# A two-layer decoder trunk on one core: the latent attention's moves between tiles leave by GpSimd's DMA queue

## The chip, the cores and the metric

The kernel runs on one core of one Trainium2 chip. A core has five instruction streams that run side by side and are tied together by semaphores: TensorE (PE, matmuls; its weight loads are listed as PEld), VectorE (DVE), ScalarE (ACT), GpSimd (POOL) and SyncE (SP). Each stream runs its instructions in the order in which the program was built. SP does no arithmetic here: it only issues DMAs. A DMA is issued by the stream on which it stands; the 16 DMA engines of the core then move the bytes.

The metric is device time in microseconds (us) of one execution of the whole program, as the median of several runs.

## The reference, cut to what matters

Two layers; in each layer one projection of the residual stream `x` (512 tokens x 1024) feeds four branches that are gated, projected, merged and normalised:

```python
for l in range(DEPTH):                      # DEPTH = 2
    h = x @ w_in[l]
    (rw_p, rw_g, q_lat, kv_lat, k_pe, mla_g, conv_u, conv_g, xq, xg, merge) = split(h)
    y_rwkv = _rwkv7_branch(...)             # recurrence, 8 heads x 64
    y_mla  = _mla_branch(q_lat, kv_lat, k_pe, mla_g, ...)
    y_conv = _conformer_conv_branch(conv_u, conv_g, ...)   # width 31
    y_mem  = _memory_xattn_branch(xq, xg, mem, ...)
    merged = sum(sigmoid(merge_n + b_n) * (y_n @ w_o_branch[l, n]) for n in 4 branches)
    x = layer_norm(alpha * x + merged @ w_out[l])
```

The branch that the change touches is the latent attention:

```python
q  = (rms_norm(q_lat) @ w_uq).reshape(S, 8, 64 + 32)     # per head: plain part, rotary part
kv = (rms_norm(kv_lat) @ w_ukv).reshape(S, 8, 64 + 64)   # per head: key part, value
q_pe, k_pe = rope(q_pe), rope(k_pe)                      # k_pe is shared by all heads
q_full = concat([q_nope, q_pe]); k_full = concat([k_nope, k_pe])      # 96 rows per head
o = causal softmax attention over 128-query blocks
```

Everything is float32. The kernel gets this accuracy from faster matmuls by splitting each operand into a high part (`h`, rounded to the float32r type) and a low part (`l`, the rest), and adding three products (`mm3`).

## The kernel before, in words

**Who decides the order.** The program is one stream of work items for PE (the projections, `stream`), into which side tasks are mixed (splitting weights, attention blocks, the convolution's taps, the recurrence). A class `Plan` keeps a clock for each engine while the program is being built. Each instruction gets a cost, and a task goes on as soon as the planner's clock of PE has reached the task's time; otherwise the next piece of the stream is put out. So the costs written into `Plan` fix the order in which instructions stand on every engine, and a change of a cost moves instructions far away from it. On the chip each engine then follows that order and waits where the planner was wrong.

**Weights.** `weights` issues one DMA of up to 128 x 1024 numbers from SP (`DMA`, which books `Plan.dma`) into one of two raw buffers (`WR = 2`), then a task splits it: ACT writes the high part, DVE the low part, into one of six pairs of tiles (`WH = 6`). The names `w0`, `w1`, ... count these pieces, so `w25h` and `w25l` are the parts of the 26th. `LOOK = 4` halves are fetched ahead. The next weights' DMA can go only when a raw buffer is free, that is, when the split of the piece that was in it has ended.

**The latent attention.** `lat_item` projects the latents, `latents` normalises and transposes them (`lt`). `key_rotary` rotates the shared key part, splits it into `krh` and `krl` and has it moved to rows 64 to 95 of the four key tile pairs `kTh`, `kTl` (8 moves in each layer). `latent_items` then makes the rotary query parts of all heads (`pqe`, `query_rotary`, transposed as `qr`, split as `qrh`, `qrl`), the values (`pv`), and four items `pair_item(hh)`, each for two heads. A pair item has the rotary parts of its queries moved to rows 64 to 95 of the query tiles `qT`, `qTl` (4 moves), computes the plain parts (`pq` for queries, `pk` for keys), and `heads` splits these (`xqh`, `xql`, `xkh`, `xkl`) and has each half moved to rows 0 to 63 of the tiles of its head (8 moves). In all 56 moves in each layer. They all go from SBUF to SBUF, since an engine's lanes keep their partitions.

When the moves of a pair are there, `pair` starts eight blocks (`mla_block`, at most three open at a time): scores `ms`, a maximum, the exponential and its sum, normalisation `mP`, transposes `mt`, a copy `mPT`, and after every four blocks the products with the values, `mo`.

**What is queued where.** Before the change, moves and weights share SP's queue. SP takes its DMAs in order: one that waits for its source, or for the DMA eight places before it that used the same semaphore, holds back those behind it. POOL runs small operations only: the reciprocal roots of the norms (`rstd_of`) and the substitution of the recurrence (`ZT`, `tmpW`).

**The convolution's norm.** `conv_norm` writes a tanh (`ctn`) into a tile of the general pool `up` (32 tiles of 128 x 512), and DVE multiplies it into `yc`. The pool `sp` has a tag `tg` with two buffers, used by the tanh of all the gates.

**Other names of the profile.** `ps_m`, `po`: projections of the merge gates and of the branches; `ps_glu`, `ps_val`, `cacc`: the convolution; `xs`, `xt`, `xo`: the cross-attention; `ps_xq`: its queries, which also go through tiles named `xqh`, `xql`; `ps_mk`, `pmv`: its keys and values; `pz`: the output projection.

Of the kernel before, what the change touches and what calls it, by code (L numbers as in the profile page):

```python
# [10 lines left out]
F32 = mybir.dt.float32  # L11
# [55 lines left out]
class Plan:  # L67
# [52 lines left out]
    def dma(self, size, outs, ins):  # L120
        t = max(self.queue, self.start("DMA", [n for n in outs if self.done.get(n, ("", ""))[1] != "DMA"], ins)) + (420.0 if ins[0][:3] == "in_" else 590.0)
        self.queue = t
        self.wires = max(self.wires, t + 650.0) + size / 360.0
        self.end("DMA", self.wires + 1500.0, outs, ins)

    def slot(self, key, bufs, name):

        q = self.slots.setdefault(key, [])
        q.append(name)
        if len(q) > bufs:  # L130
            self.done[name] = (self.seen.get(q.pop(0), 0.0), "")
# [67 lines left out]
def _names(*aps):  # L199
    return [a.tensor.name for a in aps if hasattr(a, "tensor")]  # L200
# [65 lines left out]
def trunk_kernel(ctx: ExitStack, tc: tile.TileContext, A, out, dbg=None):  # L266
    nc = tc.nc
    plan = Plan(tc.keep_in_program_order)
# [19 lines left out]
    def TR(o, i):  # L288
        plan.shape(128, 128)
        plan.op("PE", 109.0, _names(o), _names(i))  # L290
        plan.keep(nc.tensor.transpose(o, i, ident))  # L291

    def DMA(o, i, name=None):
        n = 512
        for d in o.shape[1:]:
            n *= d
        plan.dma(n, [name] if name else _names(o), _names(i))
        plan.keep(nc.sync.dma_start(o, i))

    def pool(bufs, **k):  # L300
        return Space(plan, ctx.enter_context(tc.tile_pool(bufs=bufs, **k)), bufs)
# [5 lines left out]
    sp = pool(2, name="sp")  # L307
# [18 lines left out]
    def u(name, cols=512, dt=F32, p=128):  # L326
        return up.tile([p, cols], dt, tag="u", name=name)

    def st(name, cols, bufs=8, dt=F32):
        return sp.tile([128, cols], dt, tag=f"st{cols}", name=name, bufs=bufs)  # L330
# [133 lines left out]
    def free(n=1):  # L464
        wlive["hl"] -= n
# [70 lines left out]
    HALF = [slice(0, 64), slice(64, 128)]  # L536
# [61 lines left out]
    def layer_items(l):  # L598
        items = []
        L = {}  # L600
        t_ = f"_{l}"
# [534 lines left out]
        def conv_norm():  # L1136
            ntok = []
            yield lambda: added[3] == 8
            for tb in range(4):
                ps, = yield from pa.take([128, 512], f"ct{tb}" + t_)  # L1140
                for i in range(4):
                    TR(ps[:, 128 * i:128 * i + 128], cacc[i][:, 128 * tb:128 * tb + 128])
                yield
                bs, mv = st(f"cbs{tb}" + t_, 6), st(f"cmv{tb}" + t_, 2)
                V.bn_stats(bs, ps)
                V.bn_aggr(mv, bs)
                rs = st(f"crs{tb}" + t_, 1)
                rstd_of(rs, mv[:, 1:2], 1.0, LN_EPS)
                n = u(f"cn{tb}" + t_)
                V.tensor_scalar(out=n, in0=ps, scalar1=mv[:, 0:1], scalar2=rs, op0=ALU.subtract, op1=ALU.mult)  # L1150
                pa.free()
                ntok.append(n)
                yield
            yield lambda: added[1] >= 4
            for i in range(4):
                ps, = yield from pa.take([128, 512], f"cb{i}" + t_)
                plan.due(*ntok)
                yield "pe"
                for tb in range(4):
                    TR(ps[:, 128 * tb:128 * tb + 128], ntok[tb][:, 128 * i:128 * i + 128])  # L1160
                yield
                t, z = u(f"ctn{i}" + t_), u(f"yc{i}" + t_)
                S.activation(t, ps, AF.Tanh, scale=hp("cln_g", i), bias=hp("cln_b", i))
                V.tensor_scalar(out=z, in0=ps, scalar1=pr("cln_g", i), scalar2=pr("cln_b", i), op0=ALU.mult, op1=ALU.add)
                pa.free()
                V.scalar_tensor_tensor(out=z, in0=t, scalar=1.0, in1=z, op0=ALU.add, op1=ALU.mult)
                yconv.append(z)
                yield
# [130 lines left out]
        def key_rotary():  # L1299

            kpe, ts = L["kpe"], u("rk" + t_, 256)
            k4 = kpe.rearrange("p (a d) -> p a d", a=4)
            yield lambda: angles
            rope(k4[:, :, 0:16], k4[:, :, 16:32], [ts[:, 64 * i:64 * i + 64].rearrange("p (a d) -> p a d", a=4) for i in range(4)], lambda f: f)
            ps, = yield from pa.take([128, 512], "kr" + t_)
            plan.due(kpe)
            yield "pe"
            for tb in range(4):
                TR(ps[0:32, 128 * tb:128 * tb + 128], kpe[:, 32 * tb:32 * tb + 32])
            yield  # L1310
            kr = [sp.tile([32, 512], F32R, tag="mt", name=f"kr{n}" + t_) for n in "hl"]
            yield from split(*kr, ps[0:32])
            pa.free()
            plan.due(*kr)
            yield
            for kT in L["kT"]:
                for x, y in zip(kT, kr):
                    DMA(x[64:96].bitcast(F32), y.bitcast(F32))
                plan.t += 2000.0
                yield  # L1320

# [28 lines left out]
                latT.append((h, lo))  # L1350

        ymla = []
        L["pe"] = L["pairs"] = L["jobs"] = L["turn"] = 0
        qpe, vtok = [], []

        def token_blocks(get, ks, name, cols, after):
# [59 lines left out]
        def pair_item(hh):  # L1416
            def run(get):
                wq = yield from get()
                wk = yield from get()
                there = []  # L1420
                qT = [(m(f"qT{hh}{h}" + t_, 512, "lq", 4, 96, F32R),
                       m(f"qTl{hh}{h}" + t_, 512, "qo", 1, 96, F32R) if hh % 2 > h else
                       u(f"qTl{hh}{h}" + t_, 512, F32R, 96) if hh % 2 else m(f"qTl{hh}{h}" + t_, 512, "qp", 2, 96, F32R)) for h in range(2)]
                kT = [L["kT"][2 * (hh % 2) + h] for h in range(2)]
                for h in range(2):
                    r = 64 * (hh % 2) + 32 * h
                    for x, y in zip(qT[h], qpe[hh // 2]):
                        DMA(x[64:96].bitcast(F32), y[r:r + 32].bitcast(F32), f"qTpe{hh}{h}" + t_)
                for w, ks, T, n, s in ((wq, range(3), qT, "q", MSCALE), (wk, range(3, 5), kT, "k", 1.0)):
                    ps = pp.tile([128, 512], F32, tag="pp", name=f"p{n}{hh}" + t_)  # L1430
                    for i, k in enumerate(ks):
                        c = slice(128 * i, 128 * i + 128)
                        mm3(ps, w[0][:, c], w[1][:, c], latT[k][0], latT[k][1], i == 0, k == ks[-1])
                        yield
                    free()
                    plan.spawn(heads(T, ps, n, s, there))
                plan.spawn(pair(hh, qT, kT, there))
            item([(A["w_qk"][l, hh], (384, 256))], run,
                 lambda: len(latT) == 5 and len(qpe) > hh // 2 and len(vtok) == 4 and L["pairs"] >= hh - 1 and MEM[l] is not None)

        def heads(T, ps, n, s, there):

            parts = [u(f"x{n}{x}" + t_, 512, F32R) for x in "hl"]
            S.activation(parts[0], ps, AF.Copy, scale=s)
            V.scalar_tensor_tensor(out=parts[1], in0=ps, scalar=s, in1=parts[0].bitcast(F32), op0=ALU.mult, op1=ALU.subtract)
            plan.due(*parts)
            yield
            for i, x in enumerate(parts):
                for h in range(2):
                    y = T[h][i]  # L1450
                    DMA(y[0:64].bitcast(F32), x[HALF[h]].bitcast(F32), f"{n}{i}{h}" + y.tensor.name)
                    there.append(f"{n}{i}{h}" + y.tensor.name)

        def pair(hh, qT, kT, there):
# [16 lines left out]
        def mla_block(hh, h, i, T, mo, two, done, left):  # L1471


            n = 128 * i + 128
# [18 lines left out]
                TR(ps[:, 128 * kb:128 * kb + 128], P[:, 128 * kb:128 * kb + 128])  # L1493
            yield

            if i > 1:
                PT = m("mPT" + q, 512, "mPT", 4)
            else:
                if h not in two:
                    two[h] = m("mPT" + q, 512, "mPT", 4)  # L1500
                PT = two[h][:, 128 * i:]
# [8 lines left out]
            for b in (i - i % 2, i - i % 2 + 1):  # L1510
                for kb in range(b + 1):
                    for half in range(2):
                        MM(mo[HALF[half], 128 * b:128 * b + 128], vtok[kb][:, 128 * hh + 64 * half:128 * hh + 64 * half + 64],
                           two[half, b][:, 128 * kb:128 * kb + 128], start=kb == 0, stop=kb == b)
            left[0] -= 1
            if left[0] == 0:
                L["pairs"] += 1
# [504 lines left out]
```

## Time and profile before

| | us |
|---|---|
| median of 3 runs | 1519.35 |
| lowest, highest | 1518.24, 1521.86 |
| span of the profiled execution, first to last instruction | 1518.1 |
| median less span | 1.25 |
| POOL busy, whole span | 135.8 |
| mean granted TensorE clock | 0.997 |
| DMA queue of SP | 151.65 MB in 88880 packets |

The profiled execution has no time of its own besides its span; the runs' times are taken without a profile, so the 1.25 us between span and median also hold the difference of one run from another.

How to read it: a row of the windows gives, for one stretch of time, the busy microseconds of each engine with the number of its instructions in brackets, then the granted TensorE clock as a share of full speed, the share of time in which the 16 DMA engines were busy, and GB/s. A row of the waits says who waited for whom, for how long in total, how often, and the longest. A row of the timeline starts with the start and the duration, and may end with the idle time before it and what ended that. `L235`, `L286`, `L291` and `L298` are the lines of the helpers that record each operation, each matmul, each transpose and each DMA, so instructions are told apart by their tiles: `out<-in`.

### The profile page before, as it was taken

The page shows a single profiled execution, that of the slowest core. Times are in us where ns is not written, and L with a number is a line of the kernel's source. Part 1 is how long each engine was busy: PE and PEld are TensorE (multiplying, and loading weights), DVE is VectorE, ACT ScalarE, POOL GpSimd, SP SyncE. Part 2 cuts the span into 40 slices and gives each one's busy share as a digit, 9 for nine tenths or more (in the row PEclk, how much of TensorE's full clock was granted, in tenths as well). Part 3 has the DMA queues.
Part 4 walks back from the last instruction along what each step waited for, and adds up shares of the span by engine and source line. Part 5 has one row for each costly group of instructions (what it writes and reads, how often), then busy time and mean ns, then how long its engine had stood idle before and what let it go on. Part 6 is the DMA issues. An engine that isn't in the chain of part 4 may idle for free.

```text
span 1518.1 us, 29700 instructions
## 1 busy us (share of the span) xinstructions
PE 1485.7 (98%) x11896; PEld 1238.0 (82%) x11896; DVE 1072.7 (71%) x2231; ACT 686.6 (45%) x1499; POOL 135.8 (9%) x323
## 2 busy tenths in 40 slices
PE   8999999999999999999999999999999999999997
PEld 8877788887887878888999877888887878788886
DVE  5788988765757675555554889997766586756747
ACT  5535653445245453344255556533443545443432
POOL 0000000030402021000010000000030303120002
PEclk9999999999999999999999999999999999999999
DMA  6443333322232323433343252433232323235231
GB/s 211 124 113 93 104 100 98 98 85 83 74 93 60 94 74 93 139 98 114 123 146 114 81 125 69 121 107 97 81 99 61 93 64 93 69 95 181 98 116 65
DMA packets 89018, 153.54 MB, mean 101 GB/s; under 512 B 41008, under 2 KB 47152, under 8 KB 88880
## 3 DMA queue, kind: packets, MB, share of 16 engines
q1 hardware_dynamic: 88880, 151.65, 33.9%
q8 instruction: 93, 1.52, 0.4%
q14 instruction: 45, 0.37, 0.1%
HBM read 134.32 MB, written 5.77 MB: 92 GB/s over the span
## 4 chain that ended last, share of the span: by engine, by line
PE 89%; DVE 5%; DMA 2%; ACT 2%; issue 1%; SPq 1%; POOL 0%; ACTq 0%; DVEq 0%; POOLq 0%
PE ps_m L286 22%; PE po L286 11%; PE ps_cg L286 3%; PE ps_rg L286 3%; PE ps_v L286 3%; PE ps_xg L286 3%; PE ps_mg L286 3%; PE ps_k L286 3%; PE ps_r L286 3%; PE ps_val L286 3%; PE pz L286 2%; PE ms L286 2%; PE pl L286 2%; PE ps_glu L286 2%; PE ps_xq L286 2%; PE x L286 2%
## 5 line engine op out<-in xcount | busy, mean ns | idle before, releaser
L235 DVE SCALAR_TENSOR_TENSOR cacc<-hpad,prm,cacc 128x512 f32<-128x512 f32 x240 | 178.9, 748 | 3.3
L235 ACT ACTIVATE tm<-ps_m,prm 128x512 f32<-128x512 f32 x64 | 44.1, 689 | 148.5 <-PE ps_m L286 134.7
L235 DVE SCALAR_TENSOR_TENSOR mt<-tm,po 128x512 f32<-128x512 f32 x48 | 33.0, 687 | 79.2 <-PE po L286 79.1
L235 POOL TENSOR_SCALAR ZT<-W 64x256 f32<-64x256 f32 x8 | 4.8, 600 | 621.8 <-DMA W<-scr 287.7
L235 POOL TENSOR_TENSOR ZT<-ZT,tmpW 64x14 f32<-64x14 f32 (+6 forms) x112 | 44.0, 393 | 8.8
L235 ACT ACTIVATE mP<-ms,nmm 128x512 f32<-128x512 f32 (+3 forms) x64 | 33.7, 529 | 18.3 <-DVE nmm L235 17.4
L235 POOL TENSOR_TENSOR tmpW<-ZT,W 64x14 f32<-64x14 f32 (+6 forms) x112 | 39.9, 356 | 7.9
L235 ACT COPY mPT<-mt 128x512 f32<-128x512 f32 (+3 forms) x64 | 26.7, 429 | 22.4 <-PE mt L291 17.1
L235 DVE TENSOR_TENSOR merged<-merged,mt 128x512 f32<-128x512 f32 x48 | 33.8, 704 | 1.6
L235 DVE TENSOR_REDUCE nmm<-ms 128x1 f32<-128x512 f32 (+3 forms) x64 | 29.9, 483 | 0.6 <-PE ms L286 0.2
L235 POOL TENSOR_SCALAR gr<-gm 128x8 f32<-128x8 f32 x8 | 2.3, 286 | 311.2 <-DVE gm L235 311.2
L291 PE MATMUL mt<-cst,mP 128*128 128x128 f32 x160 | 27.1, 276 | 2.6 <-DVE mP L235 2.2
L235 DVE SCALAR_TENSOR_TENSOR merged<-tm,po 128x512 f32<-128x512 f32 x16 | 11.0, 687 | 22.0 <-PE po L286 20.3
L235 DVE TENSOR_SCALAR mP<-mP,smm 128x512 f32<-128x512 f32 (+3 forms) x64 | 24.8, 387 | 2.3
L235 ACT ACTIVATE yb<-yb,mr,gr 128x64 f32<-128x64 f32 x64 | 22.1, 430 | 9.0 <-DVE mr L235 9.0
L235 POOL TENSOR_SCALAR lrs<-lmv 128x1 f32<-128x1 f32 x8 | 2.5, 315 | 263.5 <-DVE lmv L235 261.8
L291 PEld LDWEIGHTS mt<-cst,mP 128*128 128x128 f32 x160 | 18.6, 141 | 8.2 <-ACT mo L235 2.2
L235 ACT ACTIVATE z<-z,lnb,lrs 128x256 f32<-128x256 f32 (+1 forms) x16 | 9.6, 647 | 31.2 <-DVE lnb L235 31.2
L286 PE MATMUL ms<-kTl,qT 96*128 96x512 f32 (+3 forms) x64 | 22.2, 347 | 0.0
L286 PE MATMUL mo<-mPT,v 128*64 128x128 f32 x320 | 21.4, 278 | 0.5 <-ACT mPT L235 0.5
L286 PE MATMUL ms<-kTh,qT 96*128 96x512 f32 (+3 forms) x64 | 20.6, 322 | 0.0
L286 PEld LDWEIGHTS mo<-mPT,v 128*64 128x64 f32 x320 | 17.3, 136 | 4.0 <-issue 2.9
(3535 smaller groups left out, 5323.2 us busy)
## 6 DMA issues: line engine op xcount, KB each, us to landing
w<-in_w_ch_dram SPq DMA_DIRECT2D x146, 512.0 KB, 3.6
w<-in_w_o_dram SPq DMA_DIRECT2D x32, 512.0 KB, 3.6
w<-in_w_out_dram SPq DMA_DIRECT2D x16, 512.0 KB, 3.6
w<-in_w_lat_dram SPq DMA_DIRECT2D x16, 336.0 KB, 3.3
w<-in_w_mk_dram SPq DMA_DIRECT2D x8, 512.0 KB, 3.5
w<-in_w_mv_dram SPq DMA_DIRECT2D x8, 512.0 KB, 3.5
w<-in_w_qk_dram SPq DMA_DIRECT2D x8, 320.0 KB, 3.1
x<-in_xT_dram SPq DMA_DIRECT2D x8, 256.0 KB, 5.6
```

What stands on the lines that cost most here:

```text
L235: return self.plan.keep(f(*a, **k))
L286: plan.keep(nc.tensor.matmul(o, lhsT, rhs, start=start, stop=stop))
L291: plan.keep(nc.tensor.transpose(o, i, ident))
```

## The change

Four edits. `Plan` gets a second kind of DMA, `move`, which books 1000 ns on POOL's clock and lands the bytes some time after that; like `dma`, it does not order itself after other DMAs into the same tile. A function `MOVE` issues it from `nc.gpsimd`. The three places that move parts of queries and keys between tiles call `MOVE`. The tanh of the convolution's norm takes its tile from `sp`, tag `tg`. And a counter `L["values"]` counts the groups of `mo` products put out; a block waits, before it takes its tile for the transposed probabilities, until the groups of earlier pairs, and for the last block of a pair the first group of its own, have been put out.

```diff
+    def move(self, size, outs, ins):
+        t = self.start("POOL", [n for n in outs if self.done.get(n, ("", ""))[1] != "DMA"], ins) + 1000.0
+        self.clk["POOL"] = t
+        self.end("DMA", t + size / 180.0 + 1900.0, outs, ins)
...
+    def MOVE(o, i, name=None):
+        n = 512
+        for d in o.shape[1:]:
+            n *= d
+        plan.move(n, [name] if name else _names(o), _names(i))
+        plan.keep(nc.gpsimd.dma_start(o, i))
...
-                t, z = u(f"ctn{i}" + t_), u(f"yc{i}" + t_)
+                t, z = sp.tile([128, 512], F32, tag="tg", name=f"ctn{i}" + t_), u(f"yc{i}" + t_)
...
-                    DMA(x[64:96].bitcast(F32), y.bitcast(F32))
+                    MOVE(x[64:96].bitcast(F32), y.bitcast(F32))
...
-        L["pe"] = L["pairs"] = L["jobs"] = L["turn"] = 0
+        L["pe"] = L["pairs"] = L["jobs"] = L["turn"] = L["values"] = 0
...
-                        DMA(x[64:96].bitcast(F32), y[r:r + 32].bitcast(F32), f"qTpe{hh}{h}" + t_)
+                        MOVE(x[64:96].bitcast(F32), y[r:r + 32].bitcast(F32), f"qTpe{hh}{h}" + t_)
...
-                    DMA(y[0:64].bitcast(F32), x[HALF[h]].bitcast(F32), f"{n}{i}{h}" + y.tensor.name)
+                    MOVE(y[0:64].bitcast(F32), x[HALF[h]].bitcast(F32), f"{n}{i}{h}" + y.tensor.name)
...
+            if i != 2 and L["values"] < 2 * hh + i // 2:
+                yield lambda: L["values"] >= 2 * hh + i // 2
             if i > 1:
                 PT = m("mPT" + q, 512, "mPT", 4)
...
+            L["values"] += 1
             left[0] -= 1
```

In the built program 112 DMAs leave SP's list and stand on POOL's, and the order on PE, DVE and ACT differs from PE's 259th matmul row on.

## The prediction

> **What bounds the kernel now.** First the page: its busy shares, its slices and the engine shares of its chain.
>
> ```profile
> PE 1485.7 (98%) x11896; PEld 1238.0 (82%) x11896; DVE 1072.7 (71%) x2231; ACT 686.6 (45%) x1499; POOL 135.8 (9%) x323
> PE   8999999999999999999999999999999999999997
> PE 89%; DVE 5%; DMA 2%; ACT 2%; issue 1%; SPq 1%; POOL 0%; ACTq 0%; DVEq 0%; POOLq 0%
> ```
>
> PE is busy 1485.7 of 1518.1 us. The matmuls of the two programs are the same in number and kind, and in the order of the built programs PE changes between its large and its small shapes the same number of times (80 stretches of the recurrence's small matmuls, 16 of `mo`). So a gain can only come out of PE's 32.4 us of idle time and out of time at a lower clock. Where these lie, the windows show (columns: window, its length, busy us and count of PE, of the weight loads, DVE, ACT, POOL; then the granted clock, DMA share, GB/s):
>
> ```profile
> 0.00:40.00 40.00, 33.88 (x205) 33.29 (x206) 24.04 (x62) 23.88 (x56) 0.97 (x13) 1.00 0.61 200
> 40.00:80.00 40.00, 38.97 (x246) 34.87 (x245) 31.15 (x61) 22.96 (x49) 2.06 (x3) 1.00 0.42 129
> 80.00:120.00 40.00, 36.76 (x202) 31.27 (x200) 32.69 (x52) 13.16 (x27) 0.00 (x0) 0.96 0.51 133
> 120.00:160.00 40.00, 36.80 (x249) 29.73 (x250) 34.46 (x91) 23.94 (x72) 0.00 (x0) 1.00 0.34 84
> 160.00:200.00 40.00, 39.00 (x256) 31.68 (x255) 36.37 (x83) 23.80 (x63) 0.00 (x0) 1.00 0.27 71
> 880.00:920.00 40.00, 37.77 (x210) 30.53 (x209) 33.90 (x83) 22.96 (x62) 0.00 (x0) 1.00 0.48 122
> 1480.00:1520.00 40.00, 27.81 (x146) 23.82 (x144) 28.49 (x68) 8.47 (x16) 10.04 (x16) 0.89 0.18 62
> ```
>
> The first and the last window hold 6.1 and 10.3 us (38.1 - 27.8) of start and tail that no move touches. The latent attention's stretches hold 1.0 + 3.2 + 3.2 + 1.0 + 2.2 = 10.7 us. That, with the clock loss in 80 to 120, is all that the change can work on. POOL does nothing there (0.00), so the moves take no engine time from anyone; DVE is 82 to 91% busy, so part of these gaps is DVE's latency and not the queue's.
>
> Next, the waits and the time order name the gaps. Rows are of PE's waits and the sync queue's, then of the timelines of the sync queue, PE and ACT:
>
> ```profile
> PE ps_val L286 <- DVE w11l L235: 1.0, 1, 1.0
> PE pq L286 <- DVE xql L235: 2.8, 1, 2.8
> DVE yc L235 <- ACT ctn L235: 6.9, 6, 2.1
> SPq L298 <- ACT krh L235: 11.0, 1, 11.0
> 44.60 0.53 SPq L298 DMA_DIRECT2D w<-in_w_ch_dram  x1
> 33.77 1.29 DVE L235 TENSOR_TENSOR w9l<-w,w9h 128x512 fp32r<-128x512 f32 x2 [1.92 <-ACT w9h L235]
> 98.63 0.33 SPq L298 DMA_DIRECT2D w<-in_w_qk_dram  x1
> 100.10 0.33 SPq L298 DMA_DIRECT2D w<-in_w_ch_dram  x1
> 103.12 0.58 SPq L298 DMA_DIRECT2D qTl<-qrl  x1
> 106.39 0.62 ACT L235 CAST w25h<-w 128x512 fp32r<-128x512 f32 x1 [1.90 <-DMA w<-in_w_ch_dram]
> 107.22 0.59 ACT L235 ACTIVATE xqh<-pq 128x512 fp32r<-128x512 f32 x1
> 105.43 0.39 PE L286 MATMUL pk<-lth,w23l 128*128 128x512 f32 x1
> 108.59 0.79 PE L286 MATMUL pq<-ltl,w24h 128*128 128x512 f32 x1 [2.78 <-DVE xql L235]
> 109.18 0.63 PE L286 MATMUL pq<-lth,w24h 128*128 128x512 f32 x1
> 111.32 0.63 PE L286 MATMUL pq<-ltl,w24h 128*128 128x512 f32 x1
> 108.00:112.00 4.00, 3.41 (x8) 2.71 (x9) 4.00 (x7) 0.81 (x2) 0.00 (x0) 0.57 0.68 148
> 900.74 0.50 PE L286 MATMUL xo<-xPTl,vmh 128*128 128x512 f32 x1 [1.56 <-DVE xPTl L235]
> 149.56 0.41 PE L291 MATMUL mt<-cst,mP 128*128 128x128 f32 x2 [1.81 <-DVE mP L235]
> ```
>
> Two gaps trace back to moves in the sync queue. At 51 us PE waits 1.0 us for `w11`: the queue stood 11.0 us at the first rotary-key move, waiting for `krh`, and `w11` went out only behind it, at 44.60, though its raw buffer was free when `w9`'s split ended (33.77 + 1.29 = 35.1). At 105.7 PE waits 2.78 us: the next `pq` needs the bank that `xqh` and `xql` empty, `xqh` stands on ACT behind the cast of `w25`, and `w25`, issued at 100.10, was there at 106.3, with four rotary-query moves put in behind it, the last at 103.12. This gap costs twice: after it the clock is 0.57 and matmuls come every (111.32 - 109.18) / 5 = 0.43 us. The gaps at 149 and 900 end at DVE; the 1.56 us one sits behind ACT, which waited for a move to release its source.
>
> **The change, part by part.** *Off the sync queue:* 112 moves, 56 in each layer (8 key rotary parts, 16 query parts, 32 parts of heads).
>
> ```profile
> L298 SPq DMA_DIRECT2D kTh<-krh x8: 507/556/622, 43.3 to 829.0; - x8
> L298 SPq DMA_DIRECT2D kTl<-krl x8: 532/589/1278, 44.0 to 829.5; - x8
> kTh<-xkh SPq DMA_DIRECT2D x16, 128.0 KB, 4.2
> qT<-xqh SPq DMA_DIRECT2D x16, 128.0 KB, 2.3
> 43.43 1.66 POOL L235 TENSOR_TENSOR rsl<-rsl,mhalf 128x8 f32<-128x8 f32 x1
> 112.43 1.40 PE pk L286 x6
> 129.93 0.77 PE xs L286 x6
> 107.84 1.15 SPq L298 DMA_DIRECT2D qT<-xqh  x2
> ```
>
> At 0.56 us each they free 63 us of the sync queue's time, which by itself is worth nothing: weights run four pieces ahead (`LOOK`) and PE waits for them almost nowhere. What counts are the two gaps. (1) `w11` can go out up to 9.5 us sooner and must be only 1.0 us sooner: -1.0. (2) Between 98.6 and 106.3 the DMA engines carried `w24` (320 KB), `w25` (512 KB) and 4 x 64 KB of query parts. On POOL, which is idle, the query parts go out as soon as `qr` is split, in the built order some 80 matmuls earlier, so they are out of this stretch: 256 of 1088 KB less. At the 226 GB/s that the stretch of 100 to 104 moved (row below) `w25` lands 256 / 226 = 1.1 us sooner, `xqh` with it, and the gap falls from 2.78 to 1.7 us: -1.1. (3) The gap of 1.56 us in the quoted row at 900 has granted clock 1.00 after it (row below), the one of 2.78 has 0.57. A gap of 1.7 should not lower the clock: 8 matmuls at 0.43 in place of 0.23 us, -1.6.
>
> ```profile
> 100.00:104.00 4.00, 4.00 (x19) 3.34 (x18) 3.74 (x6) 0.62 (x2) 0.00 (x0) 1.00 0.84 226
> 900.00:904.00 4.00, 3.26 (x20) 2.90 (x20) 3.65 (x8) 1.22 (x3) 0.00 (x0) 1.00 0.97 245
> ```
>
> *On POOL:* the trace has no DMA issued by POOL, so its price d per move is unknown. From below: 0.33 us, the sync queue's quickest issue; from above: 1.66 us, POOL's longest instruction here. The nearest rows are the sync queue's own issues of these very moves, 0.5 to 1.28 us; I take the middle, 0.9. Nothing on POOL stands behind the moves until the recurrence's `ZT`, so only their landing counts. The tight place is the first pair of heads in each layer: in POOL's new order twelve moves go one behind the other (q, the next pair's query parts, k). In PE's new order the first `ms` stands 57 matmuls of 512 columns and 6 `xs` behind the last `pk` of that pair: 57 x 0.23 + 0.8 = 13.9 us (1.40 / 6 = 0.23). With the gap of 1.7 it comes at 105.7 + 1.7 + 13.9 = 121.3 us. The first q move can go at 107.84 - 1.1 = 106.7; the twelfth lands at 106.7 + 11 d + 4.2 (2.3 in quiet). Equal at d = 0.95, or 1.12 in quiet: about 1.0. Layer 2 has 66 + 6 `xs` + 8 transposes behind its `pq` and breaks even near 1.05. With 0.9: no wait, 0 us. Past 1.0 each tenth costs 1.1 us in each layer, and 1.6 more where the gap reaches the length that lowers the clock.
>
> The Trainium skill, SBUF — State Buffer, section "SBUF: two separate sides", says that a DMA issued from GpSimd cannot get its descriptors written while DVE runs an operation that takes both port pairs. By it, each such operation in the twelve moves' stretch adds its length. The rows below are those of 100 to 126 us that could be of this kind:
>
> ```profile
> L235 DVE TENSOR_SCALAR xP<-xP,smx 128x256 f32<-128x256 f32 x1 | 0.4, 354 | 0.0
> L235 DVE TENSOR_SCALAR mP<-mP,smm 128x128 f32<-128x128 f32 x1 | 0.3, 287 | 0.0
> ```
>
> By that rule at most 0.35 + 0.29 = 0.6 us per layer would be added and the time would be 1516.9; no trace here shows a GpSimd DMA, so it is not tested.
>
> *Two companions:* the tanh tile of the convolution's norm moves to a pool of two buffers; ACT may wait for DVE's reading of the tile before last, off PE's path, since ACT is 45% busy: 0; without that cover about as much again as DVE now waits for these tiles, 6.9 us in all. The new condition on `values` lets a block of the next pair copy its probabilities only when the pair before has issued its products; projections cover it: 0. Without cover it is a wait like the 1.81 us at 149.56, at each of the 6 changes of pairs: 10.9.
>
> *Sum:* 1518.1 - 1.0 - 1.1 - 1.6 = 1514.4 us for the span; the median run is 1519.35, 1.25 more than the profiled span, so 1515.7.
>
> **Rivals.** *No change:* DMA and DVE set these gaps, not the queue that issues. For it: DVE is 82 to 91% busy there, and `w25` needs its 512 KB in any order. Against it: the 11.0 us stand of the sync queue is plain. Only `w11`'s 1.0 remains: 1518.3. The Trainium skill, DMA: Bandwidth & Descriptors, section "Issuing engines are not separate DMA queues", says just this, that issuing from several engines saves only the sequencer's time, as all share the same 16 DMA engines; the trace agrees in so far as the freed 63 us lie under PE's work.
>
> *Slower:* d lies above 1.0 and the first `ms` of each layer waits for the twelfth move, all later PE work behind it. It decides from d = 1.0. At 1.28, the longest issue seen: 11 x 0.28 + 11 x 0.23 + 2 x 1.6 = 8.8, less 3.7: +5.1, 1524.5; at 1.66: 7.3 + 6.7 + 3.2 - 3.7 = +13.5, 1532.9. For it: the new order leaves no spare time beyond about 1 us per move, and moves on the old queue needed 0.6. Against it: nothing shows POOL that slow.
>
> *Reordering:* from the 259th matmul row on PE's order differs, and the gaps that I tie to no move of the sync queue (1.81 at 149.56, 1.0 in 160 to 200, 1.56 at 900.74, together 4.4) may close (1511.3) or come twice (1520.1). For it: DVE and ACT get a new order too; against it: the planner keeps its costs and its filling work.
>
> **How the numbers follow.** A measurement of this kernel can tell about 0.2%, 3.0 us, from no change; faster is below 1516.3, slower above 1522.4. Forecast 0.40 (own range 1512 to 1518.5; 0.34 of it faster, 0.06 within). No change 0.20 (0.02, 0.17, 0.01 slower). Slower by late moves 0.28 (0.04 within, 0.24 slower). Reordering 0.12 (0.05, 0.02, 0.05). Together faster 0.41, same 0.29, slower 0.30. The range 1508.5 to 1531 reaches from all 10.7 us gone to d near 1.6.
>
> **What would show it.** Right: PE's wait for `w11l` gone; the wait at `pq` below 2 us with the clock at 1.00 after it; POOL's moves at or below 1.0 us each; no wait of `ms` for a move. Wrong: PE idle before the first `ms` of a layer, ended by a DMA into `kTl` or `kTh`; a clock below 1.00 between 100 and 130 us; POOL's issues above 1.0 us; ACT or DVE waiting for a move's source longer than now; or the idle sum of the attention's windows unchanged at about 10.7 us.

## The result, and the profile after

The changed kernel takes 1522.59 us (median of 20 runs, 1519.84 to 1524.94), the kernel before beside it 1519.89 us (20 runs, 1517.01 to 1523.04). The ratio is 1.0017, 95% interval 1.0010 to 1.0024, so 2.6 us slower; 1515.7 was forecast. The profiled execution has a span of 1522.8 us, 4.7 above that of before; it took 1524.6 us and is among the longest of its 20 runs.

First the page of the changed kernel (engine busy times; then its new DMA queue with packets, MB and share):

```profile
PE 1487.2 (98%) x11896; PEld 1239.8 (81%) x11896; DVE 1070.5 (70%) x2231; ACT 687.6 (45%) x1499; POOL 189.6 (12%) x435
q0 software_dynamic: 4608, 11.54, 3.5%
```

POOL has 112 instructions and 54 us more. Then the windows of the changed kernel that answer to those of before:

```profile
40.00:80.00 40.00, 40.00 (x274) 36.91 (x274) 32.22 (x60) 22.66 (x50) 6.35 (x11) 1.00 0.43 129
80.00:120.00 40.00, 37.51 (x189) 30.92 (x188) 31.68 (x57) 15.50 (x30) 11.71 (x24) 1.00 0.53 137
120.00:160.00 40.00, 38.35 (x258) 30.49 (x259) 37.24 (x98) 24.86 (x77) 2.44 (x5) 1.00 0.28 75
160.00:200.00 40.00, 37.95 (x215) 30.79 (x213) 33.80 (x72) 20.63 (x52) 10.18 (x20) 0.96 0.54 126
880.00:920.00 40.00, 37.22 (x201) 30.39 (x200) 33.10 (x78) 21.88 (x58) 12.17 (x24) 0.96 0.46 113
920.00:960.00 40.00, 38.81 (x242) 30.95 (x241) 36.74 (x71) 22.70 (x53) 7.95 (x16) 1.00 0.39 106
```

In layer 1 the idle time of 40 to 160 us falls from 7.5 us to 4.1. In 160 to 200 (1.0 to 2.1) and 880 to 960 us (2.3 to 4.0) it grows, and clocks of 0.96 now stand there in place of the one in 80 to 120. Over the 36 windows from 40 to 1480 us PE is idle 13.6 us in place of 16.0. A gain of that size can't make the span longer; the end does. Here are the last instruction of DVE, which is the last work of any engine, in before and then in the changed kernel:

```profile
1514.44 0.42 DVE L235 TENSOR_TENSOR z<-z,ln_b 128x256 f32<-128x256 f32 x1
```

```profile
1513.47 0.42 DVE L240 TENSOR_TENSOR z<-z,ln_b 128x256 f32<-128x256 f32 x1
```

The changed kernel is done with its work 1.0 us sooner than before. But before ends 3.2 us later (1518.1 - 1514.9), the changed kernel 8.9 us later. Its windows there:

```profile
1514.00:1516.00 2.00, 0.00 (x0) 0.00 (x0) 0.00 (x0) 0.00 (x0) 0.00 (x0) 0.50 0.59 193
1516.00:1518.00 2.00, 0.00 (x0) 0.00 (x0) 0.00 (x0) 0.00 (x0) 0.00 (x0) 0.50 0.00 0
1520.00:1522.00 2.00, 0.00 (x0) 0.00 (x0) 0.00 (x0) 0.00 (x0) 0.00 (x0) 0.50 0.00 0
```

The last stores land by 1516, and then no engine and no DMA does anything. The views leave out semaphore and drain instructions, so the list below is from the raw records of the traces: each engine ends with a drain, reports, and waits until GpSimd answers. GpSimd's drain (listed by run, with its start, its length, and the time at which the last other engine has reported) takes 0.89 us before and 10.05 us in the changed kernel:

```
kernel                        moves by  drain  drain   others   shown of
                              GpSimd    from   us      ready    the drain
before                          0     1512.97   0.89   1517.36    0
e1_one_move                     1     1515.66   0.98   1520.03    0
e10_16_key_moves_on_pool       16     1509.57   2.21   1513.96    0
e11_32_query_moves_on_pool     32     1510.69   3.52   1515.08    0
e9_old_order_48_on_pool        48     1506.86   4.83   1511.29    0.4
e14_companions_48_on_pool      48     1505.24   4.83   1509.66    0.4
changed kernel                112     1511.99  10.05   1516.38    5.7
e15_companions_112_on_pool    112     1512.79  10.05   1517.16    5.7
e3_old_order_all_on_pool      112     1517.09  10.05   1521.47    5.7
e4_after_pool_ends_early      112     1496.96  10.00   1512.86    0
e6_new_order_act                0     1530.00   0.89   1534.39    0
```

The drain starts beside GpSimd's last instruction, and it grows by (10.05 - 0.98) / 111 = 0.082 us with each move. It goes by moves, not by bytes or packets: the 48 rotary moves carry 27% of the bytes of all 112 (3.15 of 11.54 MB) and 33% of the packets (1536 of 4608), but from one move on they add 3.85 of 9.07 us, 42%, as 47 of 111 moves do.

### The profile page after: what moved, and what is told of

Same layout as the page of the kernel before. It is cut to its first block, busy times and chain, and to the rows that moved or that the text cites. A ratio compares the mean times of both kernels' runs of the same rounds, so it can differ in the third digit from the quotient of the medians.

```text
span 1522.8 us, 29785 instructions
## 1 busy us (share of the span) xinstructions
PE 1487.2 (98%) x11896; PEld 1239.8 (81%) x11896; DVE 1070.5 (70%) x2231; ACT 687.6 (45%) x1499; POOL 189.6 (12%) x435
## 3 DMA queue, kind: packets, MB, share of 16 engines
q0 software_dynamic: 4608, 11.54, 3.5%
## 4 chain that ended last, share of the span: by engine, by line
PE 92%; DVE 3%; DMA 2%; ACT 1%; issue 1%; POOL 0%; ACTq 0%; SPq 0%; DVEq 0%; POOLq 0%
PE ps_m L291 23%; PE po L291 12%; PE ps_cg L291 3%; PE ps_xg L291 3%; PE ps_rg L291 3%; PE ps_v L291 3%; PE ps_r L291 3%; PE ps_val L291 3%; PE ps_k L291 3%; PE ps_mg L291 3%; PE ps_glu L291 3%; PE ps_xq L291 2%; PE ms L291 2%; PE pz L291 2%; PE pl L291 2%; PE x L291 2%
## 5 line engine op out<-in xcount | busy, mean ns | idle before, releaser
L240 ACT COPY mPT<-mt 128x256 f32<-128x256 f32 (+3 forms) x64 | 26.7, 427 | 17.4 <-PE mt L296 15.8
L310 POOL DMA_DIRECT2D qT<-qrh x16 | 8.0, 500 | 122.0 <-ACT qrh L240 79.7
L240 ACT ACTIVATE xP<-xs,nmx 128x256 f32<-128x256 f32 x32 | 15.2, 476 | 17.6 <-DVE nmx L240 16.7
```

The source lines that it names most:

```text
L240: return self.plan.keep(f(*a, **k))
L310: plan.keep(nc.gpsimd.dma_start(o, i))
```

## The experiments

The kernel before ran beside each group, with medians of 1520.62 (first four), 1520.95 (next four), 1521.19 (third four) and 1520.35 us (last three). The ratios are therefore the better measure; 0.001 is 1.5 us.

| run | median us | ratio, 95% interval |
|---|---|---|
| e1_one_move | 1520.63 | 0.9997 (0.9988 to 1.0006) |
| e2_new_order_sync | 1556.11 | 1.0230 (1.0214 to 1.0247) |
| e4_after_pool_ends_early | 1516.12 | 0.9969 (0.9957 to 0.9981) |
| e5_before_pool_ends_early | 1521.20 | 1.0003 (0.9992 to 1.0014) |
| e3_old_order_all_on_pool | 1531.07 | 1.0067 (1.0055 to 1.0079) |
| e6_new_order_act | 1534.05 | 1.0087 (1.0073 to 1.0101) |
| e9_old_order_48_on_pool | 1515.39 | 0.9969 (0.9957 to 0.9981) |
| e8_measured_costs_pool_ends_early | 1517.68 | 0.9987 (0.9978 to 0.9997) |
| e10_16_key_moves_on_pool | 1519.60 | 0.9993 (0.9983 to 1.0003) |
| e11_32_query_moves_on_pool | 1516.54 | 0.9969 (0.9956 to 0.9981) |
| e7_companions_alone | 1516.37 | 0.9970 (0.9956 to 0.9983) |
| e13_48_on_pool_pool_ends_early | 1516.19 | 0.9971 (0.9958 to 0.9983) |
| e14_companions_48_on_pool | 1512.61 | 0.9954 (0.9941 to 0.9966) |
| e15_companions_112_on_pool | 1525.82 | 1.0047 (1.0032 to 1.0061) |
| e16_condition_alone | 1515.09 | 0.9969 (0.9956 to 0.9983) |

### The end of the program

One move from GpSimd, in the kernel before:

```diff
-            for kT in L["kT"]:
+            for n, kT in enumerate(L["kT"]):
...
-                    DMA(x[64:96].bitcast(F32), y.bitcast(F32))
+                    if l == 1 and n == 3 and y is kr[1]:
+                        plan.dma(512 * 512, _names(x[64:96]), _names(y))
+                        plan.keep(nc.gpsimd.dma_start(x[64:96].bitcast(F32), y.bitcast(F32)))
+                    else:
+                        DMA(x[64:96].bitcast(F32), y.bitcast(F32))
```

> The kernel before with one of its 112 moves (the last key rotary move of layer 2) issued from GpSimd; the order of all other work is that of before. Theory (a fixed price at the end): once GpSimd has issued a DMA, its closing step is long, so the stretch from the end of DVE's last instruction to the end of the span grows from 3.2 us (1518.1 - 1514.9) to about 9, PE's own stretch stays, and the time is 3.7 to 5.7 us above before, 1523.6 to 1525.6. Rival (a price for each move): 1/112 of that, no change, 1519.9. Rival (the new order of PE, DVE and ACT costs the time): the order is the old one, so no change, 1519.9.

The drain is 0.98 us and the time that of before. The first form of my theory, a fixed price for any use of GpSimd's queue, fell; the rival, a price for each move, stood, and the five counts of the list above lie on its line. The runs with 16, 32 and 48 moves, expected at 2.2, 3.5 and 4.8 us, gave 2.21, 3.52 and 4.83.

The changed kernel, and the kernel before, with GpSimd's last work taken off it:

```diff
-                rstd_of(rs, mv[:, 1:2], 1.0, 16.0 * LN_EPS)
+                if last:
+                    V.tensor_scalar(out=rs, in0=mv[:, 1:2], scalar1=1.0, scalar2=16.0 * LN_EPS, op0=ALU.mult, op1=ALU.add)
+                    V.reciprocal(rs, rs)
+                    S.activation(rs, rs, AF.Sqrt)
+                else:
+                    rstd_of(rs, mv[:, 1:2], 1.0, 16.0 * LN_EPS)
...
-                    for i, eng in ((3, G), (1, V), (2, V)):
+                    for i, eng in ((3, V if tb > 1 else G), (1, V), (2, V)):
```

> The changed kernel with GpSimd's last work taken off it: the four last reciprocal roots go to DVE and ACT (reciprocal, square root), and the last two blocks' fourth pieces of the output norm to DVE, so GpSimd's last instruction ends near 1503 in place of 1512.8. Theory (a closing step of some 9 us from GpSimd's last instruction on): it runs under the tail, the stretch behind DVE's last instruction falls from 8.9 to about 3.2, and the time is 1517 to 1520, 2.5 to 5.7 below the changed kernel, more than the same edit brings in the kernel before. Rival (the closing step starts only when all engines have come to the end): no gain beyond what the edit brings in the kernel before. Rival (order or landings): the same, 1522.6 and the edit's own share.

> The kernel before with the same edit at the tail (GpSimd's last roots and pieces on DVE and ACT). It is the edit's own worth without any DMA of GpSimd. All theories: within 1.5 us of before, 1518.4 to 1521.4; two handovers of about 0.45 us between DVE and GpSimd go, 0.8 us of DVE work comes in.

The edit is worth nothing in the kernel before (1.0003) and 0.0048, 7.3 us, in the changed one (1.0017 to 0.9969; 6.5 us by the medians). That is more than the 5.7 us of the drain that stuck out, and more than the 2.5 to 5.7 expected; in the two profiled executions PE's idle time from 40 to 1480 us differs as well, 13.6 against 11.3 us, with PE's order the same. The drain is as long as ever, 10.00 us, but starts at 1496.96, when GpSimd's last instruction runs, and is over long before the others report at 1512.86. So the drain goes at its own pace behind GpSimd's last work, and the price is only what of it sticks out.

### The queue alone

All 112 moves, and the 48 rotary ones alone, from GpSimd in the old order (`MOVE` books `plan.dma` as before; in the second run the third line stays `DMA`):

```diff
+        plan.dma(n, [name] if name else _names(o), _names(i))
+        plan.keep(nc.gpsimd.dma_start(o, i))
...
-                    DMA(x[64:96].bitcast(F32), y.bitcast(F32))
+                    MOVE(x[64:96].bitcast(F32), y.bitcast(F32))
...
-                        DMA(x[64:96].bitcast(F32), y[r:r + 32].bitcast(F32), f"qTpe{hh}{h}" + t_)
+                        MOVE(x[64:96].bitcast(F32), y[r:r + 32].bitcast(F32), f"qTpe{hh}{h}" + t_)
...
-                    DMA(y[0:64].bitcast(F32), x[HALF[h]].bitcast(F32), f"{n}{i}{h}" + y.tensor.name)
+                    MOVE(y[0:64].bitcast(F32), x[HALF[h]].bitcast(F32), f"{n}{i}{h}" + y.tensor.name)
```

> The kernel before, its order on PE, DVE and ACT kept, with all 112 moves issued from GpSimd: the queue alone, without the new order and its companions. Theory (a closing step that grows with the number of moves, 0.89 us for none, 0.98 for one, 10.05 for 112): 10.0 us again, of which 5.7 stand behind the other engines' end; the gap at ps_val for w11l (1.0 us) goes and the one at pq (2.8) shrinks by about 1, so the time is 3.5 to 5 us above before, 1523.5 to 1525. Rival (the gain comes with the queue, the new order brings nothing): as the changed kernel, 1522.6. Rival (the old order is timed for quick landings; a move now needs 3.6 to 6.7 us in place of 2.3 to 4.2, and the first score of each pair waits): 2 to 3 us more for each of eight pairs in the worst case, above 1530.

> The kernel before, its order kept, with the 48 rotary moves (16 of keys, 32 of queries) issued from GpSimd and the 64 moves of heads still from SP. Theory (the closing step grows by (10.05 - 0.98) / 111 = 0.082 us for each move): 0.89 + 48 x 0.082 = 4.8 us; the other engines come to the end some 4.4 us after it starts, so only 0.4 us of it shows. Both gaps that rotary moves made in the sync queue go as in the prediction: 1519.9 - 1.0 - 1.1 - 1.6 + 0.4 = 1516.6, range 1515 to 1519. Rival (the closing step is the same for any large number of moves, 10 us): 5.7 us show, 1521 to 1523. Rival (both gaps have other causes): 1520 to 1521.

The 48 gain 0.0031 (4.7 us), 1.4 us more than expected; with the 64 moves of heads the time is 1.0067, that is 0.0098 or 15 us worse, of which the drain's 5.3 us are a third. My 1523.5 to 1525 was wrong, and the time is that of the rival of late landings (above 1530), though not every pair's first score waits. In the waits of PE of the run with 112 moves (who waited for whom, us in all, times, longest) a score waits for a move of a head, and `ps_xq` for the split of one:

```profile
PE ps_xq L286 <- DVE xql L235: 3.9, 3, 2.5
PE ms L286 <- DMA qT<-xqh: 3.2, 1, 3.2
```

The rotary moves in two halves, keys and queries:

> The kernel before, its order kept, with the 16 rotary key moves alone issued from GpSimd. It is step (1) of the prediction by itself. Theory: the closing step is 0.98 + 15 x 0.082 = 2.2 us and hidden; the gap of 1.0 us at ps_val for w11l goes, the gap at pq stays at 2 to 3 us: 1.0 us below before, 1519 to 1520. Rival (w11l is late for another reason): the gap stays, no change. Rival (slower landing of the keys makes the first score wait): above before.

> The kernel before, its order kept, with the 32 rotary query moves alone issued from GpSimd. It is steps (2) and (3) by themselves. Theory: the closing step is 0.98 + 31 x 0.082 = 3.5 us and hidden; the gap of 1.0 us at ps_val stays, the one of 2.8 at pq falls below 1.7 with the clock at 1.00 after it: 1.1 + 1.6 = 2.7 us below before, 1516.5 to 1519. Rival (the two steps do not add; the 5.5 us of the 48 moves come from the two together): within 1 us of before.

The keys alone, window of 40 to 80 us; the queries alone, two waits of PE:

```profile
40.00:80.00 40.00, 39.82 (x251) 35.58 (x249) 32.21 (x63) 23.18 (x49) 6.48 (x11) 1.00 0.39 117
```

```profile
PE ps_val L286 <- DVE w11l L235: 1.2, 1, 1.2
PE pq L286 <- DVE xql L235: 0.6, 1, 0.6
```

With the keys on GpSimd the idle 1.0 us before `w11l` is 0.2, and the time 0.9993, 1.1 us less, which this interval can't tell from nothing. The gap at `pq`, expected at 2 to 3 us, is 1.8 there (and 2.1 and 2.5 in the two runs below that move nothing to GpSimd), so without any query move on GpSimd it lies anywhere between 1.8 and 2.8. With the queries on GpSimd that gap stays and the one at `pq` is 0.6 us; the time is 0.9969, 4.7 us less, more than the 2.7 expected. The two add up to what the 48 gain (5.8 against 4.7 us) within these intervals of some 2 us; more can't be said.

The version of 48 with GpSimd's last work off it:

> The version with the 48 rotary moves on GpSimd in the old order, and GpSimd's last work taken off it as in the earlier runs of that kind. Theory: the closing step of 4.8 us, of which about 0.6 showed, is hidden altogether, and the edit itself is worth 0: 1514.2 to 1515.8. Rival (what showed of the closing step is nothing, and the edit costs some tenths): 1515.4 to 1516.5.

0.9971 against 0.9969: the 0.4 us of the drain can't be seen in the time, which is the rival's (1516.2).

### The new order

The changed kernel with `nc.sync.dma_start`, and with `nc.scalar.dma_start`, in `MOVE`; order and booking stay:

```diff
-        plan.keep(nc.gpsimd.dma_start(o, i))
+        plan.keep(nc.sync.dma_start(o, i))
```

> The changed kernel's order on PE, DVE and ACT and its two companions, with the 112 moves issued from SP again. Theory (a fixed price at the end of using GpSimd's queue): the stretch behind DVE's last instruction is 3.2 us again, and the time is at most 1.5 us from before on either side, 1518.4 to 1521.4; the 1.0 us gap at ps_val for w11l is back. Rival (the new order costs the time): as the changed kernel, 1522.6. Rival (the queue's slower landings cost it): below before, 1517 or less, since the new order then has quick landings.

> The changed kernel's order with the 112 moves issued from ScalarE in place of GpSimd. Theory (the closing step belongs to GpSimd's own DMA work): its closing step is 0.9 us again and the stretch behind DVE's last instruction 3.2 us, 5.7 less than in the changed kernel; against that ACT, 45% busy, gets 112 issues of about 0.5 us and stands while one waits for its source, so the rest of the time lies 0 to 10 us above the changed kernel's: 1517 to 1527. Rival (the closing step belongs to the moves, whoever issues them): the stretch stays at 8.9 us and the time is above 1522.6.

Both cost far more than I expected, 35 and 13 us above the kernel before. The drain is 0.89 us in both, so it belongs to GpSimd's own moves. The new order, as I read these two runs, needs a queue in which the moves stand in nobody's way. On SP the moves stand before the weights again; the waits of the sync queue and a window of PE in that run:

```profile
SPq L310 <- ACT krh L240: 22.2, 2, 11.5
SPq L310 <- ACT w32h L240: 16.2, 1, 16.2
200.00:240.00 40.00, 35.55 (x222) 28.51 (x220) 31.44 (x75) 20.33 (x59) 0.00 (x0) 0.91 0.32 89
```

From ScalarE it is the projections' banks that come free late: in that run the longest of PE's waits inside the program is

```profile
PE ps_xq L291 <- DVE xql L240: 10.9, 2, 6.1
```

The changed kernel with GpSimd's last work off it and the moves booked nearer to what they took:

```diff
-        t = self.start("POOL", [n for n in outs if self.done.get(n, ("", ""))[1] != "DMA"], ins) + 1000.0
+        t = self.start("POOL", [n for n in outs if self.done.get(n, ("", ""))[1] != "DMA"], ins) + 510.0
...
-        self.end("DMA", t + size / 180.0 + 1900.0, outs, ins)
+        self.end("DMA", t + size / 180.0 + 3600.0, outs, ins)
```

> The changed kernel with its tail relieved of GpSimd's last work, as in the run before of that kind, and with the moves booked in the planner as they were measured: 510 ns on GpSimd in place of 1000, and 1.7 us more until they land. Theory (the rest of the gaps comes from the planner's wrong landings): PE's idle time outside the first and the last stretch falls below the 11.2 us of that run, and the time below 1516.1, to 1512 to 1515. Rival (those gaps come from DVE's and ACT's latencies, which no booking of moves changes): within 1.5 us of 1516.1. Rival (any new order brings its own gaps): above 1517.6.

PE's idle time between 40 and 1480 us is 11.0 us as against 11.3 with the old booking, and the time is 0.9987 (0.9978 to 0.9997) as against 0.9969 (0.9957 to 0.9981): no gain. The intervals overlap, so whether the new order lost anything (the third line of the expectation) or changed nothing (the second) is open. Truer costs alone didn't make a better order.

### The companions

The two companions without any move on GpSimd, and the condition alone (the order on every engine is the same in both):

```diff
-                t, z = u(f"ctn{i}" + t_), u(f"yc{i}" + t_)
+                t, z = sp.tile([128, 512], F32, tag="tg", name=f"ctn{i}" + t_), u(f"yc{i}" + t_)
...
+            if i != 2 and L["values"] < 2 * hh + i // 2:
+                yield lambda: L["values"] >= 2 * hh + i // 2
...
+            L["values"] += 1
```

> The kernel before with the two companions alone (the tanh of the convolution's norm from the pool with two buffers, the condition on the groups of value products), all moves from SP. They were booked at 0. Theory: within 1.5 us of before, 1519 to 1522. Rival (the condition moves instructions and brings gaps of its own like that of 1.8 us at mt): 2 to 6 us above before.

> The kernel before with the condition on the groups of value products alone, the tanh tile as before. The order on all engines is that of the two companions together. Theory (the gain comes from the new order, which the condition makes): as the two together, 1515 to 1518. Rival (the gain comes from the tanh tile, DVE's wait for ctn of 6.9 us): as before, 1520 to 1521.5.

I had booked them at nothing, and neither my 1519 to 1522 nor the rival's loss came. They bring 0.0030, and the condition alone 0.0031, 4.6 and 4.7 us: it is the condition. It holds blocks back until the products of earlier pairs are out, and so changes the order from the place of the 1.81 us gap on. The windows of the run with both companions there (3.2 and 1.0 us idle before; with the condition alone PE is busy 39.53 and 39.95 us):

```profile
120.00:160.00 40.00, 38.79 (x257) 30.69 (x256) 36.83 (x97) 25.41 (x77) 0.00 (x0) 1.00 0.37 93
160.00:200.00 40.00, 39.94 (x260) 32.50 (x259) 36.40 (x80) 24.45 (x62) 0.00 (x0) 1.00 0.34 90
```

The companions with 48 moves, and with all 112, on GpSimd, in the companions' order (`MOVE` as in the runs with the queue alone):

> The kernel before with the two companions and the 48 rotary moves on GpSimd, in the order that the companions alone give; the 64 moves of heads from SP. Theory (the gains are different gaps: the companions close those at mt and in 120 to 200 us, the rotary moves those at ps_val and pq): 1516.4 - 1.0 - 1.1 - 1.6 + 0.4 = 1513.1, range 1511.5 to 1514.8. Rival (they close the same gaps, or a gap closed here opens there): 1515 to 1517. Rival (the closing step of 4.8 us shows more than 0.4): above 1516.

> The kernel before with the two companions and all 112 moves on GpSimd, in the order that the companions alone give: the changed kernel without its new booking. Theory (the moves of heads are what gives the gain back, as they land 2 to 4 us later from GpSimd and the booking only softens that): the closing step of 10.0 us shows 5.7, and scores and their banks wait for moves; as in the old order (1531.1 with 112 moves, 1515.4 with 48, 10.6 of the difference not the closing step) the time lies at 1526 to 1532. Rival (the booking's order gives it back): below the changed kernel, 1517 to 1521.

The companions and the 48 moves together give 0.9954, 1512.6 us, 7.0 us below before and 9.6 below the changed kernel, the fastest of all that were run, where 1513.1 was expected. Alone they brought 4.6 and 4.7 us; whether all of that 9.3 adds, these intervals don't tell. The 64 moves of heads then cost 0.0093, 14 us, just below the theory's range (1525.8 as against 1526 to 1532). Windows of layer 2 and waits of PE, first with 48 moves, then with 112:

```profile
880.00:920.00 40.00, 38.41 (x233) 30.76 (x232) 33.57 (x83) 22.49 (x64) 1.98 (x4) 0.96 0.47 117
920.00:960.00 40.00, 39.95 (x242) 31.60 (x241) 37.03 (x78) 21.54 (x57) 2.08 (x4) 1.00 0.48 121
PE ps_xq L286 <- DVE xql L235: 0.4, 1, 0.4
```

```profile
880.00:920.00 40.00, 36.86 (x233) 30.04 (x232) 33.89 (x82) 22.80 (x62) 12.16 (x24) 1.00 0.47 115
920.00:960.00 40.00, 37.23 (x201) 29.54 (x200) 31.92 (x65) 18.76 (x50) 10.17 (x20) 0.91 0.46 109
PE ps_xq L286 <- DVE xql L235: 3.1, 2, 2.7
PE ms L286 <- issue: 2.7, 1, 2.7
PE ms L286 <- DMA kTl<-xkl: 1.8, 1, 1.8
```

The drain's 5.3 us, 6.4 us more of idle time between 40 and 1480 (13.6 against 7.2) and some 2 us more of lost clock ((0.96 - 0.91) x 40) make up the difference. Of the two waits of scores the longer stands in layer 2, at 950.93; the view names no releaser for it ("issue").

How such a gap comes about is seen best in the changed kernel itself. The rows are of DVE, ACT, PE and POOL in layer 2, in order of time within each engine:

```profile
889.48 0.69 DVE L240 SCALAR_TENSOR_TENSOR xql<-pq,xqh 128x512 fp32r<-128x512 f32 x1 [2.47 <-DMA qTl<-xql]
890.33 0.60 ACT L240 ACTIVATE xkh<-pk 128x512 fp32r<-128x512 f32 x1 [2.28 <-DMA qT<-qrh]
890.22 0.50 PE L291 MATMUL ps_xq<-xl,w147h 128*128 128x512 f32 x1 [2.79 <-DVE xql L240]
883.86 1.03 POOL L310 DMA_DIRECT2D qTl<-xql  x2
889.64 0.52 POOL L310 DMA_DIRECT2D kTl<-xkl  x1 [1.10 <-DMA qTl<-xql]
884.00:888.00 4.00, 3.44 (x15) 2.46 (x14) 2.98 (x8) 2.72 (x8) 3.87 (x8) 1.00 0.97 266
```

The second pair's `xql` takes over the tile from which the first pair's `qTl` moves read. These went out from 883.86 to 884.9, but the DMA engines were full just then (0.97, 266 GB/s: further moves, and a 512 KB piece of weights that SP issued at 884.11), and they landed at about 889.4. DVE stood 2.5 us with everything behind it, ACT 2.3 us until a rotary move had landed, the bank of `pq` stayed taken, and PE stood 2.8 us. This cause is read from the trace; what is shown by experiment, in the companions' order, is that with the moves of heads back on SP the wait at `ps_xq` falls from 3.1 to 0.4 us and those of scores go.

## Why the prediction was wrong

*The step that failed* is the sentence of the part on POOL, "Nothing on POOL stands behind the moves until the recurrence's `ZT`, so only their landing counts". GpSimd's closing drain stands behind them, 0.082 us for each, 9.2 us for 112, of which 5.7 stick out at the program's end. The sum had no term for the end. With +5.7 alone its -3.7 would have been +2.0, and +2.6 was measured; but that closeness is partly chance, as three more terms were missing (-4.6, +8.8 and -4.6 below) which nearly cancel.

The change part by part, each as a difference of measured ratios, uncertain by some 2 us, but for the drain, which is read from the traces (5.7 - 0.4):

| part | booked | measured |
|---|---|---|
| companions | 0 | -4.6 (0.9970) |
| 48 rotary moves to GpSimd, on top | -3.7 with the next | -2.4 (0.9954) |
| 64 moves of heads to GpSimd, drain left out | | +8.8 |
| closing drain, 112 moves less 48 | 0 | +5.3 |
| the planner's booking of `move` | 0 | -4.6 (1.0047 to 1.0017) |
| whole change | -3.7 | +2.6 |

- *(1) `w11`, -1.0:* right. The gap is 0 in the changed kernel and 0.2 with the keys alone; the time of that run, 0.9993, fits, though its interval takes in no change.
- *(2) the gap at `pq`, -1.1:* right in kind. The gap is 1.3 us in the changed kernel, where 1.7 was forecast, and 0.6 us with the queries alone, a run worth 4.7 us in the old order.
- *(3) the clock, -1.6:* in 80 to 120 us it is 1.00 as forecast, but not for the reason given. The length of 1.56 us was taken as one that leaves the clock alone, since it was 1.00 behind the gap at 900.74. With the keys alone the same gap has a lowered clock right behind it:

```profile
896.01 0.50 PE L286 MATMUL xo<-xPTl,vmh 128*128 128x512 f32 x1 [1.56 <-DVE xPTl L235]
896.00:900.00 4.00, 3.99 (x12) 3.25 (x12) 2.67 (x4) 1.18 (x2) 0.00 (x0) 0.58 1.00 299
```

  So a gap of that length may lower the clock or not. The changed kernel has two windows at 0.96 elsewhere, and the run with the queries alone has one in 120 to 160 us: the loss moved, and the 1.6 us isn't shown as a gain.
- *The price of a move:* 0.9 us was taken; it is 0.50 to 0.55 for all but three of the changed kernel's moves, and 0.73 at most (rows of two kinds: count; minimum, median, maximum in ns). The rival of late moves, which needed more than 1.0, fell: no score waits for a move there. The slower side came true by another way.

```profile
L310 POOL DMA_DIRECT2D qT<-xqh x16: 516/520/533, 105.7 to 957.9; - x16
L310 POOL DMA_DIRECT2D kTh<-krh x8: 496/517/727, 45.4 to 825.3; - x8
```

- *Landings:* taken as on SP, 2.3 to 4.2 us. For the moves of heads they are 3.6 to 6.7 in the changed kernel (KB each, median us to landing). The last row is the `qTl` move from ScalarE, in the same order of work:

```profile
qTl<-xql POOLq DMA_DIRECT2D x16, 128.0 KB, 5.0
kTh<-xkh POOLq DMA_DIRECT2D x16, 128.0 KB, 5.8
qTl<-xql ACTq DMA_DIRECT2D x16, 128.0 KB, 5.4
```

  From SP, again in that order, `qTl` takes 2.3. So long landings aren't GpSimd's alone; I read them from the full DMA engines in the window above, where moves and weights run side by side. Whether GpSimd adds to them is open (`kTl` takes 6.7 from it and 4.8 from ScalarE).

- *The moves of heads:* none of the gaps that the prediction summed was theirs, and they were moved along at no price. In the old order and in the companions' order they lose 9 to 10 us beside the drain; the booking's order gives half of it back. I had looked for a late landing before the first score, and not at the tiles that the moves keep from being written.
- *Two readings,* which no term hangs on: in 40 to 80 us POOL is busy 2.06 us, not 0.00, and DVE 78% (31.15 of 40), where 82 to 91% is said.
- *The companions:* "projections cover it: 0" failed, on the good side. The rival of reordering had named the gaps that close (1.81 at 149.56 and 1.0 in 160 to 200) and priced them, with that at 900.74, at 4.4; the condition alone closes those two (2.8 together), and the time fell 4.7.
- *No change,* the rival by which DVE and the DMA engines set these gaps whatever queue issues, fell: the queries' moves alone shrink the gap at `pq` to 0.6 us, well below the 1.8 to 2.8 without them, and the time falls 4.7 us.
- *The two rules of the Trainium skill:* "SBUF — State Buffer", section "SBUF: two separate sides", would have shown as moves that take longer beside DVE's two-port operations. No issue of a move of a head on POOL is over 0.53 us, with DVE 79 to 92% busy in the windows of 40 us that hold them; no row tells which of DVE's operations there were of that kind, and whether some of the landings are longer for it is not told apart here. "DMA: Bandwidth & Descriptors", section "Issuing engines are not separate DMA queues", says that all issuers share the same DMA engines: the long landings agree. Its conclusion that only the sequencer's time is saved is too narrow here, since what 48 rotary moves no longer hold back in SP's queue is worth 4.7 us.

## What to carry to other kernels

Before moving DMAs to GpSimd, count them and look at what GpSimd does last: its closing drain took 0.082 us for each here, and cost nothing where GpSimd's last work came that much ahead of the other engines' end. Move only the transfers that hold up others in a queue (here 48 of 112, whose sources come late), and leave those there whose landing frees a tile that is wanted next (the second half of this rests on one gap read from the trace). A change of a queue that drags a new order along is four changes: run the order, the queue and its companions apart, as here the best of them (1512.6 us) was hidden in a sum that came out slower.

## What was unexpected in the hardware

GpSimd's closing drain: 0.89 us with no DMA of its own, 0.98, 2.21, 3.52, 4.83 and 10.05 us with 1, 16, 32, 48 and 112, whatever their size (64 or 128 KB) and although the last of them had gone out some 540 us earlier or more. A move issued by GpSimd occupied it for 0.50 to 0.55 us (0.73 at most), and the 64 KB key moves landed sooner from it than from SP (median 2.0 us with 48 moves on GpSimd, 2.6 and 3.4 in the changed kernel, 3.8 and 3.5 before). A gap of PE of 1.56 us had a clock of 0.58 behind it in one run and 1.00 in another.
